# Mixture of experts: experts ranked by token count, the four smallest on 64 slots in plain float32, inputs fetched by indirect DMA

## The chip, the cores and the metric

One core of one Trainium2 chip runs the whole program. The metric is device time in microseconds for one execution, the median over several.

## The reference, cut to what matters

256 tokens of width 1024 go through two blocks of two layers each. All data is float32. What matters here is the second feed-forward part of the first block: a router picks 2 of 8 experts for each token, and each expert is a SwiGLU with 3584 hidden units.

```python
def moe_swiglu(h, router_w, router_b, w_gate, w_up, w_down):
    logits = h @ router_w + router_b
    top_vals, top_idx = lax.top_k(logits, 2)
    top_w = softmax(top_vals)
    combine = sum(one_hot(top_idx, 8) * top_w[..., None], axis=-2)
    y = 0
    for e in range(8):
        y = y + combine[..., e:e+1] * ((silu(h @ w_gate[e]) * (h @ w_up[e])) @ w_down[e])
    return y
```

The weights of one expert are 3 x 1024 x 3584 float32 numbers, 44.04 MB; those of all eight are 352 MB. The router's counts on the inputs that the reference draws (seed 0) are 66, 67, 71, 64, 49, 57, 54 and 84 tokens for experts 0 to 7, 512 in all.

The second block has a stream of its own over a context of 256 tokens. Its first layer does not depend on the first block, so it can be computed beside it.

## The kernel before, in words

The program is a set of generators ("tasks") that issue instructions; a scheduler then orders each engine's instructions by priority. The main stream has the key "lead", the context's first layer (task `B` in `plan`) the key "fill" with a far lower priority: what it issues fills the places where the lead is not ready. Each task takes its buffers from its own set of pools (`Res`). While `B` runs, the lead's experts use `RM`: four weight buffers w0, split buffers h0, h2 and w2, PSUM t0 and a0. `B` uses `RF`: w1, h1, PSUM a1 and t1. `plan` runs the expert generator until it yields "alone" and then gives it all weight buffers (`RN`); from there nothing fills. "alone" stands in the third expert (number 2), just before its last unit. So two and nine tenths experts run beside `B`, and five and one tenth after it.

The precise products are made of three passes. A weight tile arrives by one DMA of 512 KB (`wload`, L211, issued by the queue SP, 128 rows of 4 KB). `split` (L295) makes of it a rounded high part in float32r on ACT (L296) and the rest on DVE (L297). `mm3` (L228) then issues three float32r products: high x high (L234), high x low (L239), low x high (L240).

`moe` (L747) normalizes the tokens, computes the logits, picks the top two by vector operations, and ranks the tokens of each expert by products with a triangle of ones, which gives each token its slot (`pos`). If an expert has more than 128 tokens, the branch at L824 runs `overflow` for slots 128 and up. `experts` (L893) then takes the eight experts in their order. `gather(e)` makes one-hot matrices from the slots (L903), multiplies the normalized tokens by them (L909, plain float32, 16 products of 128 columns), applies scale and shift (L915, L917) and splits the result. `unit(u)` multiplies the 128 gathered slots (stationary) by 512 columns of gate and up weights over 8 blocks of k: 24 passes of 512 columns. 14 units make an expert; `down` adds 28 blocks of k times two column halves: 168 passes. With 14 x 24 that is 504 passes of 512 columns and 84 loads of 512 KB (56 for gate and up, 28 for down) for each expert. `scatter` (L882) adds the result to the tokens by a product with the one-hot rows.

Plain float32 is used elsewhere in the kernel: the modulation (L388, L410) and the convolution (L689) put four products of 32 output rows side by side on the column groups of TensorE. In the trace a plain float32 product has two records for each instruction of the program.

Of the kernel before, what the change touches and what calls it, by code (L numbers as in the profile page):

```python
# [9 lines left out]
F32 = mybir.dt.float32  # L10
F32R = mybir.dt.float32r
# [6 lines left out]
P = 128  # L18
D = 1024
T = 256  # L20
# [26 lines left out]
CC_SPEC = [("ident", 128), ("ones", 128), ("tri", 128), ("iota", 128), ("rev8", 8), ("psum", 32), ("pick1", 4), ("pick2", 8)]  # L47
# [15 lines left out]
class Res:  # L63
    """buffers of one stream: pools to take each kind of tile from (the listed ones in turn)"""
# [14 lines left out]
class Task:  # L79
    """a generator of instructions with its buffers and its place in the order of issue"""  # L80
# [15 lines left out]
class Builder:  # L96
    def __init__(self, tc, A, out, es, taps=None):
# [23 lines left out]
        self.RF = Res(w[1:2], h[1:2], a1, a1, a1, a1, t1, s1, s1, s1, s1, k[1], g[1], m[1])  # L121
        self.RM = Res(w[:1], hm, t0, a0, a0, a0, t2, s3, s2, s2, s3, k[0], g[0], m[0])
# [94 lines left out]
    def wparts(self, dram):  # L217
        """loads dram [128, kt, n]; yields (first k, its k count, high part, low part), 4 KiB a part"""
# [28 lines left out]
    def half_rsqrt(self, h, w):  # L247
        """1 / sqrt(2 h): three Newton steps, each of which turns the sign, from a negative guess"""
# [36 lines left out]
    def rstd_rows(self, xs):  # L285
        """xs[t][n] [128,512] token-major; 1/rms per token, [128, 1] for each t"""
# [24 lines left out]
    def affine_f32(self, ps, kp, Aff, Bff, pool=None):  # L311
        """ps [128, 2, w] -> A*ps+B"""
# [21 lines left out]
    def scaled_t(self, xs, r):  # L334
        """channel-major xs * r, two blocks of channels at a time: products with diagonals of r"""
# [18 lines left out]
    def conds(self):  # L354
        """silu of the three conditions, [128, 8, 32]: second block's two, first block's, zeros"""
# [16 lines left out]
    def gemv_step(self, m, c, A, name, l, grow):  # L372
        """a twelfth of the 6144 columns, in four column groups of the tensor engine"""
# [6 lines left out]
    def shift_scale(self, m, b, q, w_dram):  # L380
        """128 columns of each half of shift and scale: a column group each, then to channels on partitions"""
# [45 lines left out]
    def affine(self, m, which, i, gname):  # L427
        """(A, B) of g * (1 + scale), shift; which 0: mixer, 1: ffn"""
# [13 lines left out]
    def proj_parts(self, H, w, n, evac, kind="a"):  # L442
        """token-major [2 x 128, n] = H^T-stationary product with w [128, 8, n], in parts"""
# [19 lines left out]
    def ffn(self, H, gu, dn, nu, part, size=2):  # L463
        """SwiGLU over 256 tokens; part(section, t, n, psum) gets the product of each section of the hidden units"""
# [5 lines left out]
        def unit(u):  # L470
            """hidden units on partitions: gate and up blocks of 128, two of each to a bank"""
# [72 lines left out]
    def mixer1(self, l, H, M):  # L544
# [10 lines left out]
        # convolution branch, channels on partitions  # L555
# [30 lines left out]
        # gating branch  # L586
# [26 lines left out]
        # gating products  # L613
# [25 lines left out]
        # convolution, layer norm over channels, swish  # L639
# [107 lines left out]
    def moe(self, xs, m):  # L747
        nc, A = self.nc, self.A
        Aff, Bff = self.affine(m, 1, 0, "gf1")
        V, S, ones = nc.vector, nc.scalar, self.cc("ones")  # L750
# [7 lines left out]
        for t in range(2):  # L758
# [3 lines left out]
            V.tensor_add(lg[:, t], ps, rb)  # L762

# [39 lines left out]
        tri = self.cc("tri")  # L803
        for t in range(2):
# [6 lines left out]
        ps = self.ms(8)  # L811
        for t in range(2):
            nc.tensor.matmul(ps, ones, sel[:, t], start=t == 0, stop=t == 1)
        mx = self.m1(1)
        V.tensor_reduce(mx, ps, AX.X, ALU.max)
        cnt = cp.tile([P, 1], I32, name="cnt")
        V.tensor_copy(cnt, mx)
        self.tap("cw", cw)
        self.tap("pos", pos)
        G = [self.gate_bc(m, 5, 0, n) for n in range(2)]  # L820
        pos2 = cp.tile([P, 2, 8], F32, name="pos2")
        V.tensor_scalar(pos2, pos, 128.0, None, op0=ALU.subtract)
        nmax = nc.values_load(cnt[0:1, 0:1], min_val=0, max_val=256)
        with self.tc.If(nmax > 128):  # L824
            r, self.R = self.R, self.R0
            self.overflow(xn, Aff, Bff, pos2, cw, G, xs)
            self.R = r
        yield
        yield from self.experts(xn, Aff, Bff, pos, cw, G, xs)

    def overflow(self, xn, Aff, Bff, pos, cw, G, xs):
        """slots 128..255 of each expert, in the buffers of the weights alone"""
        nc, A = self.nc, self.A
        V, S, idn, iota = nc.vector, nc.scalar, self.cc("ident"), self.cc("iota")
        for e in range(8):
            mt = self.shaped(self.htile(), (8, 128))
            Dt, DT, act = mt[:, 0:2], mt[:, 2:4], mt[:, 4:8]
            Df = Dt.bitcast(F32)
            for t in range(2):
                V.tensor_scalar(Dt[:, t], iota, pos[:, t, e:e + 1], None, op0=ALU.is_equal)  # L840
            Xh, Xl = (self.shaped(self.tile(self.R.turn("w"), 1024, F32R), (8, 128)) for _ in range(2))
            for k in range(8):
                ps = self.tp(128)
                for t in range(2):
                    nc.tensor.matmul(ps, xn[t][k // 4][:, (k % 4) * 128:(k % 4 + 1) * 128], Df[:, t],
                                     start=t == 0, stop=t == 1)
                hf = self.g1(128)
                V.tensor_scalar(hf, ps, Aff[:, k:k + 1], Bff[:, k:k + 1], op0=ALU.mult, op1=ALU.add)
                self.split(Xh[:, k], Xl[:, k], hf)
            pd = self.tp(2, 128)  # L850
# [1027 lines left out]
```

## Time and profile before

| | us |
|---|---|
| median of three runs | 2912.77 (2910.46, 2912.77, 2920.75) |
| profiled execution: span | 2917.1 |
| PE busy | 2771.0 (95%) |
| DVE busy | 2025.3 (69%) |
| ACT busy | 1700.4 (58%) |
| DMA | 711.71 MB, mean 244 GB/s |

The page gives the span of the profiled execution, from its first to its last instruction, and no separate time for it; the span is 4.3 us over the median of the runs. PE is the matrix engine and PEld its weight loads, DVE the vector engine, ACT the scalar engine, POOL the general engine, SP the queue that issues loads. Records of products are about 0.17 us longer than the place they take on PE, since a product drains while the next one streams; the pace is read from their starts.

### The profile page before, as it was taken

The page shows a single profiled execution, that of the slowest core. Times are in us where ns is not written, and L with a number is a line of the kernel's source. Part 1 is how long each engine was busy: PE and PEld are TensorE (multiplying, and loading weights), DVE is VectorE, ACT ScalarE, POOL GpSimd, SP SyncE. Part 2 cuts the span into 40 slices and gives each one's busy share as a digit, 9 for nine tenths or more (in the row PEclk, how much of TensorE's full clock was granted, in tenths as well). Part 3 has the DMA queues.
Part 4 walks back from the last instruction along what each step waited for, and adds up shares of the span by engine and source line. Part 5 has one row for each costly group of instructions (what it writes and reads, how often), then busy time and mean ns, then how long its engine had stood idle before and what let it go on. Part 6 is the DMA issues. An engine that isn't in the chain of part 4 may idle for free.

```text
span 2917.1 us, 46050 instructions
## 1 busy us (share of the span) xinstructions
PE 2771.0 (95%) x17334; PEld 2295.3 (79%) x17334; DVE 2025.3 (69%) x3099; ACT 1700.4 (58%) x2353; POOL 77.8 (3%) x144
## 2 busy tenths in 40 slices
PE   6999999998899999999999999998999999799898
PEld 5767788776788888887878888876667989677897
DVE  3535555656777878789899998985566555666555
ACT  3435445545566666666777777775445554654543
POOL 0110000010000000000000000000000000000000
PEclk8999999999999999999999999999989999899999
DMA  9987766642688888888999999996563556324463
GB/s 358 338 298 234 250 198 225 222 127 84 224 307 296 295 282 299 298 290 313 350 354 339 350 347 360 355 361 210 167 211 110 182 171 189 118 66 132 152 185 112
DMA packets 202954, 711.71 MB, mean 244 GB/s; under 512 B 24506, under 2 KB 28730, under 8 KB 202720
## 3 DMA queue, kind: packets, MB, share of 16 engines
q1 hardware_dynamic: 196112, 692.82, 69.6%
q0 software_dynamic: 6320, 15.30, 1.8%
q8 instruction: 138, 2.26, 0.3%
q14 instruction: 96, 0.79, 0.1%
q10 hardware_dynamic: 288, 0.55, 0.1%
HBM read 704.49 MB, written 4.08 MB: 243 GB/s over the span
## 4 chain that ended last, share of the span: by engine, by line
PE 65%; DVE 3%; ACT 2%; DMA 2%; issue 1%; DVEq 0%; SPq 0%; ACTq 0%; POOLq 0%
PE a0t L234 8%; PE a0t L239 8%; PE a0t L240 8%; PE a1t L239 6%; PE a1t L240 6%; PE a1t L234 6%; PE t0t L239 5%; PE t0t L240 5%; PE t0t L234 5%; PE a1t L1512 1%; PE t0t L1535 1%; ACT h0t L296 1%; DVE h0t L297 1%; PE t0t L344 1%; PE t2t L909 1%
## 5 line engine op out<-in xcount | busy, mean ns | idle before, releaser
L296 ACT CAST h0t<-w0t 128x1024 fp32r<-128x1024 f32 (+1 forms) x505 | 525.4, 1043 | 386.1 <-PE a0t L239 243.8
L297 DVE TENSOR_TENSOR h0t<-w0t,h0t 128x1024 fp32r<-128x1024 f32 (+1 forms) x302 | 364.9, 1209 | 264.7 <-ACT h0t L296 247.5
L234 PE MATMUL a0t<-s0t,h0t 128*128 128x256 f32 x800 | 225.9, 287 | 4.4 <-ACT h0t L296 2.1
L239 PE MATMUL a0t<-s0t,h0t 128*128 128x256 f32 x800 | 224.2, 284 | 0.0
L240 PE MATMUL a0t<-s0t,h0t 128*128 128x256 f32 x800 | 220.1, 286 | 0.5 <-DVE h0t L297 0.5
L296 ACT CAST h1t<-w1t 128x1024 fp32r<-128x1024 f32 x155 | 162.9, 1051 | 96.1 <-PE a1t L239 44.6
L239 PE MATMUL a0t<-h0t,s2t 128*128 128x512 f32 x492 | 193.8, 396 | 0.0
L240 PE MATMUL a0t<-h0t,s2t 128*128 128x512 f32 x466 | 181.0, 394 | 0.0
L297 DVE TENSOR_TENSOR h2t<-w0t,h0t 128x1024 fp32r<-128x1024 f32 x122 | 149.1, 1222 | 29.9 <-ACT h0t L296 22.3
L234 PE MATMUL a0t<-h0t,s2t 128*128 128x512 f32 x466 | 167.4, 399 | 1.0 <-DVE s0t L1176 0.5
L234 PEld LDWEIGHTS a0t<-s0t,h0t 128*128 128x128 f32 x800 | 153.0, 192 | 13.1 <-issue 4.5
L296 ACT CAST h0t<-w1t 128x1024 fp32r<-128x1024 f32 x120 | 126.2, 1052 | 49.4 <-PE a1t L240 17.4
L239 PEld LDWEIGHTS a0t<-s0t,h0t 128*128 128x128 f32 x800 | 153.6, 192 | 1.6 <-issue 0.8
L240 PEld LDWEIGHTS a0t<-s0t,h0t 128*128 128x128 f32 x800 | 150.0, 192 | 4.2 <-DVE h0t L297 1.9
L234 PE MATMUL t0t<-h0t,s0t 128*128 128x512 f32 x374 | 147.1, 393 | 1.9 <-ACT h0t L296 1.9
L239 PE MATMUL t0t<-h0t,s0t 128*128 128x512 f32 x372 | 147.7, 397 | 1.3 <-DVE h0t L297 1.3
L240 PE MATMUL t0t<-h0t,s0t 128*128 128x512 f32 x374 | 147.5, 394 | 0.0
L297 DVE TENSOR_TENSOR h1t<-w0t,h0t 128x1024 fp32r<-128x1024 f32 x81 | 98.9, 1221 | 25.1 <-ACT k0t L483 6.6
L297 DVE TENSOR_TENSOR h1t<-w1t,h1t 128x1024 fp32r<-128x1024 f32 x80 | 97.7, 1222 | 23.9 <-ACT h1t L296 21.8
L239 PE MATMUL a1t<-s1t,h1t 128*128 128x256 f32 x408 | 113.7, 283 | 0.0
L234 PE MATMUL a1t<-s1t,h1t 128*128 128x256 f32 x408 | 113.4, 283 | 0.0
L297 DVE TENSOR_TENSOR h0t<-w0t,h1t 128x1024 fp32r<-128x1024 f32 x80 | 97.7, 1221 | 20.0 <-ACT k0t L483 5.0
(740 smaller groups left out, 7453.2 us busy)
## 6 DMA issues: line engine op xcount, KB each, us to landing
w0t<-in_mgu_dram SPq DMA_DIRECT2D x306, 512.0 KB, 5.5
w0t<-in_mdn_dram SPq DMA_DIRECT2D x152, 512.0 KB, 5.2
w1t<-in_mgu_dram SPq DMA_DIRECT2D x107, 512.0 KB, 5.7
w0t<-in_f2gu_dram SPq DMA_DIRECT2D x66, 512.0 KB, 3.9
w1t<-in_f2gu_dram SPq DMA_DIRECT2D x61, 512.0 KB, 4.8
w1t<-in_win_dram SPq DMA_DIRECT2D x54, 512.0 KB, 4.9
w1t<-in_mdn_dram SPq DMA_DIRECT2D x54, 512.0 KB, 5.4
w1t<-in_mod_s_dram SPq DMA_DIRECT2D x48, 512.0 KB, 6.2
```

Of the source, the lines that this page charges most:

```text
L234: i = mm(ps, lh, rh, start=start if skip else first, stop=False, skip_group_check=skip)
L239: mm(ps, lh, rl, start=False, stop=False, skip_group_check=skip)
L240: mm(ps, ll, rh, start=False, stop=last, skip_group_check=skip)
L296: self.nc.scalar.copy(out_h, src)
L297: self.nc.vector.tensor_sub(out_l, src, out_h)
L344: self.nc.tensor.matmul(ps[:, q, t * 128:(t + 1) * 128], xs[t][k // 4][:, (k % 4) * 128:(k % 4 + 1) * 128], dg[:, t], start=True, stop=True)
L909: nc.tensor.matmul(ps[:, q], xn[t][k0 // 4][:, q * 128:q * 128 + 128], Dt[:, t], start=t == 0, stop=t == 1)
L1512: nc.tensor.matmul(pe[:, h].rearrange("p a b -> p (a b)"), x[:, (h0 + h) * 128:(h0 + h + 1) * 128], rhs, start=i == 0, stop=i == 1)
L1535: nc.tensor.matmul(ps[:, h], L[:, h], R[:, h], start=True, stop=True)
```

## The change

The count of each expert is computed first, and the experts are put in order of their counts (a rank by comparing 8 x 8 numbers; the expert's own number breaks ties). Slots and weights are permuted into that order. The eight expert numbers go to eight registers of SP, and every expert load takes its address from such a register. Whatever has more tokens than its place allows (64 for the first four, 128 for the others) goes to the overflow branch.

The inputs are no longer gathered by one-hot products. The affine result of all tokens (`keep`) is transposed back to rows, stored to DRAM, and each expert fetches its rows by an indirect DMA on POOL, with the token numbers as indices. `G2` is the output gate in two halves of 64 partitions.

The four smallest experts (`expert64`) use plain float32 products with no split. Their 64 slots are the stationary operand; two blocks of 512 columns go at the same time to output partitions 0 to 63 and 64 to 127. Their loads go in turn to w0 and h0, four buffers each (`RS`). "alone" now stands before the fifth expert. The other four (`expert128`) are `unit` and `down` as before, with register addresses.

```diff
+        self.RS = Res([w[0], h[0]], h[:1], t0, a0, a0, a0, t2 + a0, s3, s2, s2, s3, k[0], g[0], m[0])
...
     def moe(self, xs, m):
-        r = self.rstd_rows(xs)
-        keep = [self.affine_f32(ps, kp, Aff, Bff, self.xpools[0]) for kp, ps in enumerate(self.scaled_t(xs, r))]
-        xn = self.xnorm(xs, r, self.xpools[0])
+        keep = [self.affine_f32(ps, kp, Aff, Bff, self.xpools[0])
+                for kp, ps in enumerate(self.scaled_t(xs, self.rstd_rows(xs)))]
...
+        self.hrow = [self.dram(T) for _ in range(2)]
+        for t in range(2):
+            for n in range(2):
+                ps = self.tp(4, 128)
+                for q in range(4):
+                    k = 4 * n + q
+                    nc.tensor.transpose(ps[:, q], keep[k // 2][:, k % 2, t * 128:t * 128 + 128], idn)
+                y = self.s2(4, 128, pool=self.xpools[0])
+                if n:
+                    S.copy(y, ps)
+                else:
+                    V.tensor_copy(y, ps)
+                nc.gpsimd.dma_start(self.hrow[n][t * 128:t * 128 + 128], y.rearrange("p a b -> p (a b)"))
...
+        V.scalar_tensor_tensor(n8, pc, 8.0, self.cc("rev8"), op0=ALU.mult, op1=ALU.subtract)
+        V.tensor_tensor(less, n8[:, None, :].to_broadcast(b8), n8[:, :, None].to_broadcast(b8), op=ALU.is_lt)
+        V.tensor_reduce(rank, less, AX.X, ALU.add)
+        V.tensor_tensor(perm, rank[:, None, :].to_broadcast(b8), i8[:, :, None].to_broadcast(b8), op=ALU.is_equal)
+        def ranked(out, v):
+            V.tensor_tensor(j, perm, v[:, None, :].to_broadcast(b8), op=ALU.mult)
+            V.tensor_reduce(out, j, AX.X, ALU.add)
+        ranked(f8, i8)
+        V.tensor_copy(eid, f8)
+        ranked(c8, cnt8)
+        V.tensor_sub(c8, c8, caps)
...
+            ranked(pos_r[:, t], pos[:, t])
+            ranked(cwt[:, t, :, 0], cw[:, t])
...
+        _, eids = nc.values_load_multi_w_load_instructions(eid[0:1, 0:8], engines=(mybir.EngineType.SP,), min_val=0, max_val=7)
+        nmax = nc.values_load(cnt[0:1, 0:1], min_val=0, max_val=512)
         with self.tc.If(nmax > 128):
+            self.overflow(eids, pos2, cwt, G, xs)
...
+    def slots(self, pos, cwt, r, width, Dt=None):
+        for t in range(2):
+            V.tensor_scalar(o, i0, pos[:, t, r:r + 1], None, op0=ALU.is_equal)
+        for t in range(2):
+            nc.tensor.matmul(pw, Dt[:, t].bitcast(F32), cwt[:, t, r], start=t == 0, stop=t == 1)
...
+    def fetch(self, out, n, idx):
+        self.nc.gpsimd.indirect_dma_start(out=out, out_offset=None, in_=self.hrow[n][:, :],
+            in_offset=bass.IndirectOffsetOnAxis(ap=idx[:out.shape[0]], axis=0))
...
+    def inputs64(self, idx):
+        for n in range(2):
+            g = self.s2(512)[:64]
+            self.fetch(g, n, idx)
+            for q in range(4):
+                self.nc.tensor.transpose(ps[:, 4 * n + q], g[:, q * 128:q * 128 + 128], self.cc("ident")[:64, :64])
+        self.nc.scalar.copy(X, ps)
...
+    def expert64(self, reg, X):
+        gu, dn = self.expert("mgu", reg), self.expert("mdn", reg)
+        def units(p):
+            ps = self.acc(512)
+            for k0 in range(0, 8, 2):
+                w = [self.wload(gu(2 * p + g, slice(None), slice(k0, k0 + 2))) for g in range(2)]
+                for j in range(2):
+                    for g in range(2):
+                        nc.tensor.matmul(ps[64 * g:64 * g + 64], X[:, k0 + j], w[g][:, j],
+                                         start=k0 + j == 0, stop=k0 + j == 7)
+            a = self.glu_evac(ps)
+...
+        def down(p):
+            for i in range(4):
+                w = self.wload(dn(slice(None), slice(k, k + 1)))
+                for n in range(2):
+                    nc.tensor.matmul(pn[0][64 * n:64 * n + 64], act[p][:, q, 64 * g:64 * g + 64],
+                                     w[:, 0, n * 512:n * 512 + 512], start=k == 0, stop=k == 27)
+        for p in range(7):
+            units(p)
+            if p: down(p - 1)
+            if p == 3: yield "next"
+        down(6)
...
-        moe = task(self.moe(xs, m[1]), RM)
+        moe = task(self.moe(xs, m[1]), self.RS)
```

In `experts`, `if r == 4: yield "alone"` stands where the test for expert 2 stood. `ranked(c8, cnt8)` gives the counts in the new order. `slots` makes the one-hot rows of a rank and from them the weight and the token number of each slot. The label "next" is where the next expert's slots and inputs are issued. The scatter of a small expert is one weighted copy of 512 columns and four plain float32 products on 64 rows.

## Rows read from the trace of the kernel before

**Rows 1.** Windows: us, then busy us (records) by engine, granted clock, DMA share, GB/s.
```profile
757.00:1303.00 546.00, 542.15 (x2978) 468.95 (x2979) 435.62 (x494) 365.87 (x452) 0.00 (x0) 0.99 0.87 293
1303.00:1330.00 27.00, 23.20 (x97) 18.71 (x96) 22.00 (x29) 16.16 (x24) 1.07 (x2) 0.94 0.84 280
1330.00:1951.00 621.00, 615.42 (x2821) 502.06 (x2820) 571.17 (x647) 475.38 (x590) 0.00 (x0) 1.00 0.96 350
```

**Rows 2.** DMA issues from 757 to 1303: count, KB each, us to landing.
```profile
w0t<-in_mgu_dram SPq DMA_DIRECT2D x164, 512.0 KB, 5.4
w0t<-in_mdn_dram SPq DMA_DIRECT2D x79, 512.0 KB, 4.9
w1t<-in_f2gu_dram SPq DMA_DIRECT2D x40, 512.0 KB, 5.5
w1t<-in_f2dn_dram SPq DMA_DIRECT2D x22, 512.0 KB, 5.0
```

**Rows 3.** Groups by form, 757 to 1303: the context stream's passes, one of three lines each.
```profile
L239 PE MATMUL a1t<-s1t,h1t 128*128 128x256 f32 x352 | 97.8, 283 | 0.0
L239 PE MATMUL a1t<-h1t,s1t 128*128 128x512 f32 x76 | 29.8, 392 | 0.7 <-DVE h1t L297 0.7
```

**Rows 4.** Timeline of PE: start, us, instruction; split passes at 320 and at 1500.
```profile
319.82 0.28 PE L239 MATMUL a0t<-s0t,h0t 128*128 128x256 f32 x1
319.94 0.28 PE L240 MATMUL a0t<-s0t,h0t 128*128 128x256 f32 x1
...
1499.84 0.39 PE L239 MATMUL a1t<-h2t,s0t 128*128 128x512 f32 x1
1500.07 0.39 PE L240 MATMUL a1t<-h0t,s0t 128*128 128x512 f32 x1
```

**Rows 5.** Timeline of PE from 2194: plain float32 over the whole width.
```profile
2194.37 1.98 PE L1625 MATMUL t0t<-k0t,s1t 128*128 128x512 f32 x4
2196.19 0.38 PE L1575 MATMUL t1t<-s1t,s0t 128*128 128x128 f32 x2
```

**Rows 6.** Windows, records of L689 alone: four column groups in plain float32.
```profile
640.00:650.00 10.00, 9.99 (x150) 5.70 (x138) 1.00 0.63 194
```

**Rows 7.** Timeline of PE from 2043: column groups between whole-width passes.
```profile
2043.86 0.39 PE L240 MATMUL a0t<-h0t,s1t 128*128 128x512 f32 x1
2044.09 0.61 PE L234 MATMUL a0t<-h0t,s1t 128*128 128x512 f32 x2
2044.63 0.64 PE L410 MATMUL a1t<-w1t,conds 128*32 128x256 f32 x8
2045.20 0.50 PE L239 MATMUL a0t<-h1t,s1t 128*128 128x512 f32 x1
2045.54 0.39 PE L240 MATMUL a0t<-h0t,s1t 128*128 128x512 f32 x1
2045.77 0.39 PE L234 MATMUL a0t<-h0t,s1t 128*128 128x512 f32 x1
```

**Rows 8.** Windows, 20 to 40 us.
```profile
20.00:40.00 20.00, 15.65 (x181) 10.40 (x184) 5.11 (x29) 3.06 (x9) 0.00 (x0) 0.51 1.03 408
```

**Rows 9.** Waits of the queue SP, 757 to 1303: total us, times, longest.
```profile
SPq L211 <- DVE h0t L297: 170.2, 118, 4.0
SPq L211 <- DVE h2t L297: 107.8, 76, 3.5
```

**Rows 10.** Lines L211 and L823 on SP: duration ns min/median/max.
```profile
L211 SPq DMA_DIRECT2D w0t<-in_mgu_dram x164: 327/328/949, 757.0 to 1292.9; - x164
L823 SPq TENSOR_LOAD <-cnt x1: 464/464/464, 749.8 to 749.8; - x1
L823 SPq FUSED_REGOPS  x1: 186/186/186, 750.3 to 750.3; - x1
```

**Rows 11.** Timeline of DVE at 741: two operations of the router.
```profile
741.49 0.17 DVE L799 TENSOR_TENSOR m0t<-m0t,m0t 128x16 f32<-128x16 f32 x1
741.82 0.18 DVE L801 TENSOR_TENSOR cw<-cw,m0t 128x16 f32<-128x16 f32 x1
```

**Rows 12.** DMA issues of the whole span on POOL's queue.
```profile
s0t<-dt POOLq DMA_DIRECT2D x10, 256.0 KB, 4.0
dt<-s3t POOLq DMA_DIRECT2D x4, 256.0 KB, 5.0
```

**Rows 13.** Chain of waits, 757 to 1303: start, us, half of one gather.
```profile
866.19 1.78 PE t2t L909 x16
```

More of the change, by code (lines that the diff above doesn't have):

```diff
@@ L824, in moe @@
+        _, eids = nc.values_load_multi_w_load_instructions(
+            eid[0:1, 0:8], engines=(mybir.EngineType.SP,), min_val=0, max_val=7,
+            skip_runtime_bounds_check_because="the experts' numbers in another order")
+        nmax = nc.values_load(cnt[0:1, 0:1], min_val=0, max_val=512)
         with self.tc.If(nmax > 128):
             r, self.R = self.R, self.R0
-            self.overflow(xn, Aff, Bff, pos2, cw, G, xs)
+            self.overflow(eids, pos2, cwt, G, xs)
             self.R = r
@@ L828, in moe, with expert @@
         yield
[L829 to L835, printed above, removed]
+        yield from self.experts(eids, pos_r, cwt, G, G2, xs)
+    def expert(self, name, reg):
+        w = self.A[name]
+        return lambda *i: w[(bass.ds(reg, 1), *i)].rearrange("o p k n -> (o p) k n")
+    def slots(self, pos, cwt, r, width, Dt=None):
+        nc, V = self.nc, self.nc.vector
+        Dt = self.s2(2, 128) if Dt is None else Dt
+        i0 = self.cc("iota")[:, 0:width]
+        for t in range(2):
+            o = Dt[:, t]
+            if width == 64:
+                o = o.rearrange("p (a b) -> p a b", a=2)
+                i0 = self.cc("iota")[:, None, 0:64].to_broadcast([P, 2, 64])
+            V.tensor_scalar(o, i0, pos[:, t, r:r + 1], None, op0=ALU.is_equal)
+        pw = self.tp(2)
+        for t in range(2):
+            nc.tensor.matmul(pw, Dt[:, t].bitcast(F32), cwt[:, t, r], start=t == 0, stop=t == 1)
+        w = self.m1(3)
+        V.tensor_copy(w[:, 0:1], pw[:, 0:1])
+        V.tensor_scalar(w[:, 1:2], pw[:, 1:2], 1.0, None, op0=ALU.subtract)
+        V.tensor_scalar(w[:, 2:3], pw[:, 1:2], 129.0, None, op0=ALU.subtract)
+        idx = self.m1(1, I32)
+        V.tensor_scalar(idx, pw[:, 1:2], 1.0, 0.0, op0=ALU.subtract, op1=ALU.max)
+        return w, idx
@@ new lines, in rows_at, with overflow @@
+    def rows_at(self, DT, w):
+        for t in range(2):
+            self.nc.vector.tensor_scalar(DT[:, t], self.cc("iota"), w[:, 1 + t:2 + t], None, op0=ALU.is_equal)
+    def fetch(self, out, n, idx):
+        self.nc.gpsimd.indirect_dma_start(
+            out=out, out_offset=None, in_=self.hrow[n][:, :],
+            in_offset=bass.IndirectOffsetOnAxis(ap=idx[:out.shape[0]], axis=0))
+    def overflow(self, eids, pos, cwt, G, xs):
+        nc = self.nc
+        V, S, idn = nc.vector, nc.scalar, self.cc("ident")
+        for r in range(8):
+            gu, dn = self.expert("mgu", eids[r]), self.expert("mdn", eids[r])
@@ L836, in overflow @@
             mt = self.shaped(self.htile(), (8, 128))
[L837 to L840, printed above, removed]
+            DT, act = mt[:, 2:4], mt[:, 4:8]
+            w, idx = self.slots(pos, cwt, r, 128, mt[:, 0:2])
+            self.rows_at(DT, w)
+            Xg = self.wtile()
             Xh, Xl = (self.shaped(self.tile(self.R.turn("w"), 1024, F32R), (8, 128)) for _ in range(2))
[L842 to L849, printed above, removed]
@@ new lines, in experts, with ready @@
+    def experts(self, eids, pos, cwt, G, G2, xs):
+        def ready(r):
+            small = r < 4
+            w, idx = self.slots(pos, cwt, r, 64 if small else 128)
+            DT = self.s2(2, 128, dt=F32 if small else F32R)
+            self.rows_at(DT, w)
+            return (self.inputs64 if small else self.inputs128)(idx), DT, w[:, 0:1]
+        nxt = ready(0)
+        for r in range(8):
+            if r == 4:
+                yield "alone"
+            X, DT, ws = nxt
+            steps = self.expert64(eids[r], X) if r < 4 else self.expert128(eids[r], X)
+            for at in steps:
+                if at == "next":
+                    if r < 7:
+                        nxt = ready(r + 1)
+                elif at is None:
+                    yield
+                else:
+                    pn = at
+            if r < 4:
+                y = self.s2(512)
+                self.nc.vector.scalar_tensor_tensor(y, pn, ws, G2, op0=ALU.mult, op1=ALU.mult)
+                for t in range(2):
+                    for n in range(2):
+                        ps, sl = self.ms(512), slice(64 * n, 64 * n + 64)
+                        self.nc.tensor.matmul(ps, DT[sl, t], y[sl], start=True, stop=True)
+                        self.nc.vector.tensor_add(xs[t][n], ps, xs[t][n])
+            else:
+                for n in range(2):
+                    yh, yl = self.st(512, dt=F32R), self.st(512, dt=F32R)
+                    self.scatter(pn[n], ws, G[n], self.s2(512), yh, yl, DT, xs, n)
+            yield
@@ L978, in experts @@
             yield
+            if p == 3:
+                yield "next"
+        down(6)
+        yield pn
     def setup(self):
```

205 lines of the change are left out of this document (107 added, 98 removed).

## The prediction

> **What bounds the kernel now.** I read the windows first, since the change touches one stretch only. From 757 us, where the first expert load is issued, to 1303, where the second mode with all buffers begins, PE is busy for 542 of 546 us, DMA 0.87 of its time and DVE 436 us [rows 1]. So the stretch in which the context stream fills the gaps of the experts is bound by PE. From 1330 to 1951 PE is busy for 615 of 621 us, DMA 0.96 and DVE 571: PE first, with DMA and DVE close behind [rows 1]. The DMA issues say what each stretch carries: 243 expert loads (164 and 79) and 62 of the context up to 1303 [rows 2]. Of the 672 loads of eight experts (84 each) 429 are left for the 648 us from 1303 to 1951: 1.51 us a load, 127 us an expert. The waits of SP show the loads waiting mostly for the DVE half of a split, which frees the weight buffer [rows 9]: the loads follow the products, not the other way round. Everything outside 757 to 1951 stays as it is.
>
> I go through three stretches: the router, stage 1 (experts beside the context stream) and stage 2 (experts alone). The sum is made against the profiled execution's 2917.1 us. That is 4.3 us, or 0.15%, over the median of 2912.8, and I take the difference over to the median. About 0.5%, 15 us, is what a measurement of this kernel can tell from no change.
>
> **Router.** Before SP can load an expert number, the change adds a chain of about 8 small DVE operations (comparison, two reductions, permutation, copies) at 0.18 us with their gaps 0.2 each [rows 11]: 1.6 us. The check of the counts, slots and weights in the new order add some 16, 3.2 us, on the same in-order engine. Eight register loads on SP at 0.46 [rows 10] would be 3.7 us. Sixteen transposes at 0.11 (16 records in 1.78 us [rows 13]) are 1.8 us of PE, and four copies lie beside them on DVE and ACT. The four scalings of the normalized tokens go. The ends are 2 us, if the chain lies beside the transposes, and 15, if all is in series; I take 7: loads begin at 764. The first inputs need a row store (5.0 us) and then a fetch (the direct read of a row in DRAM takes 4.0 us [rows 12]). An indirect one is not in the trace; between 4 and 10 us. During it up to eight weight buffers fill, 4 MB or some 11 us of DMA, so it costs nothing while the loads stay the bound; without that cover at most 10 us, once. Later fetches are issued half an expert ahead. POOL is idle throughout both stages but for two issues [rows 1].
>
> **Stage 1, DMA.** It now carries four experts and the same context work: 336 + 62 = 398 loads, 208.7 MB. The loads of a small expert have eight buffers, and these are freed by products instead of splits. At the 350 GB/s of the stretch from 1330, divided by its share 0.96 [rows 1], DMA gives 365 GB/s: 572 us. The ends are 596 us at 350 itself, and 527 us at 396 (408 GB/s at a share of 1.03 from 20 to 40 us [rows 8], where many loads stand ready). I take 572: the same weights in the same 4 KB rows.
>
> **Stage 1, PE.** A split product of 512 columns is paced at 0.227 us a pass, one of 256 at 0.12 [rows 4]. The context has 3 x 352 of 256 and 3 x 76 of 512 [rows 3]: 127 + 52 = 179 us. A big expert would need 504 x 0.227 = 114 us. A small one has 112 + 56 = 168 plain float32 products. The trace shows these at full width: four records, two products, from 2194.37 to 2196.19 [rows 5], 0.91 us each. One alone would make 168 x 0.91 = 153 us, more than the split expert. All hangs on whether the two column halves run at once. No row has halves of 64, but the convolution has quarters of 32: 150 records of 256 columns in 10 us, 67 ns each [rows 6], against 228 if one came after another (half of 455 [rows 5]). So 3.4 of 4 run at once. The bounds for an expert are then 76 us (two at once) and 153 (one after another); I take 80, near the row with the quarters. Four make 320 us. Transposes and scatter add about 26 products' records at 0.11 and four at 0.91, 6.5 us an expert, 26 in all. PE: 320 + 179 + 26 = 525 us, under the 572 of DMA.
>
> One rule speaks against the change. Where a batch of eight column records stands between whole-width passes, the stretch from 2044.63 to 2045.54 holds 0.46 us of column work (two rounds of 0.228) and one pass of 0.227 [rows 7]: 0.22 us are left over. The Trainium skill, "TensorEngine Tiling (Array Packing)", section "Key Properties", says that a change of the tiling mode, not only of the tile, drains TensorE; the row agrees. A small expert comes in 28 groups for gate and up and 28 for down, so at most 56 such excursions, 12 us an expert and 49 in all. By the row PE then needs 525 to 574 us.
>
> ACT and DVE lose 84 splits an expert at about 1.05 and 1.22 us, and neither was first here; the release of their time counts for nothing beyond the loads that no longer wait for it. What is late next is DMA, with PE right behind. Two engines within 10% of their bound don't cover each other wholly: I take 590 us for stage 1, 18 above the DMA term.
>
> **Stage 2.** Four big experts at 127 us are 508. Each loses its gather of 32 records at 0.11 (3.6 us) for eight transposes (0.9): 2.7 us of a PE that is 99% busy, 11 in all; nothing if DMA takes over, which at 365 GB/s needs 121 us an expert. I take 497. The loads' register addresses cost SP perhaps three register operations of 0.19 beside the issue of 0.33 [rows 10], about 1.0 us with a wait, below 1.48 (590 / 398) and 1.5 us: hidden.
>
> **Sum.** Last expert load at 764 + 590 + 497 = 1851 instead of 1951: 100 us less. Forecast 2817 for the profiled execution, 2813 for the median.
>
> **Rivals.** First, the fill bunches up. The order on PE's queue is written ahead, and lead products go first. If the schedule takes the small experts for busier on PE than they are, the context's work is put late, and from the fifth expert on the lead needs w1, h1 and a1, which the context holds until its end. The lead's own 176 MB take 483 us; with all 179 us of the context behind them stage 1 is 662, with half of it (527 us of loads, then 90) 617. Time 2840 to 2885; 2865 as one number. For it: two streams with a fixed order; against it: before, the context's passes run through the whole of stage 1 with PE 99% busy [rows 1]. Second, stage 1 goes better: loads at the 396 GB/s [rows 8] and few excursions, 540 us, 2763. For it: eight buffers and no split in the way; against it: PE needs 525 without any switch.
>
> Third, the other side: the halves run one after another, as [rows 5]. Then PE needs 4 x 153 + 179 + 26 = 817 us in stage 1, the end is 127 us later, 3040. It decides above 0.72 us a product (1951 - 764 - 497 = 690; less 205, over 672 products), between the 0.48 taken and 0.91. For it: no row has halves; against it: [rows 6]. Fourth, SP: at 2 us a load instead of 1.0, 398 and 336 loads need 796 and 672 us, about 3190; against it [rows 10]. Fifth, the change doesn't keep to its places: the reference's four smallest counts are 49, 54, 57 and 64, so the fourth is full. One token more by another rounding, and the branch runs all experts again: 8 x 127 = 1016 us more, over 3800.
>
> **How the numbers follow.** Forecast 0.57 (its own range 2785 to 2840), bunched fill 0.20, better 0.10, halves in series 0.07, SP 0.02, overflow 0.02, and 0.02 for no change by pieces of these. Faster by over 0.5%: 0.87; within: 0.02; slower: 0.11. The range for 8 in 10 leaves out the slower cases: 2765 to 2885.
>
> **What will show it.** Right: pairs of 64-column records that start within some ns of each other, and a pace near 0.46 us for a pair of passes; DMA share in stage 1 at 0.95 or more at 350 to 380 GB/s, SP waiting for PE instead of DVE; the first load of the fifth expert near 1355; the context's passes spread up to that point; stage 2 at 124 us an expert. Wrong: column records in series; a stretch before the fifth expert in which only the context's passes run while DMA idles; SP issuing back to back with no waits; expert loads after the eighth expert.

## The result, and the profile after

| | us |
|---|---|
| before, median of 4 runs beside the changed kernel | 2911.61 (2909.69 to 2920.75) |
| after, median of 4 runs | 2845.28 (2842.21 to 2845.92) |
| ratio | 0.9762, 95% interval 0.9747 to 0.9778 |
| forecast | 2813 (2765 to 2885) |
| span of the profiled execution after | 2844.0 |

The change saves 66 us where 100 were forecast, and the time is 32 us above the forecast of 2813. It lies 5 us above the forecast's own range (2785 to 2840) and inside the interval of the first rival (2840 to 2885). To find the 32 us, look first at when each expert's first load is issued, since the loads follow the products. These times are the starts of the load instructions in the trace:

| first load of expert, us | 1 | 2 | 3 | 4 | 5 | 6 | 7 | 8 | last load |
|---|---|---|---|---|---|---|---|---|---|
| before | 757 | 935 | 1129 | 1322 | 1452 | 1578 | 1704 | 1831 | 1951 |
| after | 757 | 932 | 1128 | 1278 | 1387 | 1512 | 1637 | 1761 | 1882 |

Stage 1 (from 757 to the first load of the fifth expert) took 630 us, 40 more than forecast. Stage 2 took 495 (forecast 497), and the loads began at 757, not 764. So the whole miss lies in stage 1: 2813 + 40 - 2 - 7 = 2844.

The windows of the changed kernel answer to [rows 1]. The columns are the same: us, busy us (records) of PE, PEld, DVE, ACT and POOL, granted clock, DMA share, GB/s.

```profile
757.00:1215.00 458.00, 451.34 (x2215) 243.46 (x2217) 127.86 (x186) 103.21 (x143) 7.96 (x8) 0.99 0.89 309
1215.00:1388.00 173.00, 161.78 (x598) 48.97 (x596) 24.03 (x57) 14.28 (x35) 3.12 (x4) 1.00 1.01 393
1388.00:1882.00 494.00, 486.80 (x2166) 386.04 (x2165) 444.61 (x497) 366.32 (x451) 12.45 (x6) 1.00 0.98 362
```

Stage 1 has two parts with different bounds. Up to 1215 the context runs beside the small experts, PE is busy for 451 of 458 us and DMA has room (0.89). The context's last product comes at 1227; from there the small experts are by themselves, and DMA is full (1.01). DMA was forecast to bound the whole of stage 1. It bounds only the end of it; PE bounds the rest, as before the change (the run e1_pair below shows it).

What PE does in that time is read from the timeline (start us, duration, engine, line, instruction). L1052 is the gate and up product of a small expert; `w0t` and `h0t` hold the weights of its two column halves. L236, L241 and L242 are the three passes of a split product (the lines 234, 239 and 240 of before). The first line is the indirect fetch on POOL (L923).

```profile
759.74 1.01 POOL L923 DMA_INDIRECT s3t<-dt,m0t  x1 [10.04 <-DVE m1t L278]
...
773.18 0.64 PE L1052 MATMUL t0t<-w0t,s0t 128*64 128x512 f32 x1 [0.24 <-ACT s0t L1024]
773.18 0.64 PE L1052 MATMUL t0t<-h0t,s0t 128*64 128x512 f32 x1
773.66 0.59 PE L1052 MATMUL t0t<-w0t,s0t 128*64 128x512 f32 x1
773.66 0.59 PE L1052 MATMUL t0t<-h0t,s0t 128*64 128x512 f32 x1
774.09 0.59 PE L1052 MATMUL t0t<-w0t,s0t 128*64 128x512 f32 x1
774.09 0.59 PE L1052 MATMUL t0t<-h0t,s0t 128*64 128x512 f32 x1
...
1002.80 0.59 PE L1052 MATMUL t0t<-h0t,s0t 128*64 128x512 f32 x1
1002.81 0.59 PE L1052 MATMUL t0t<-w0t,s0t 128*64 128x512 f32 x1
1003.23 1.02 PE L1052 MATMUL t0t<-h0t,s0t 128*64 128x512 f32 x2
1004.18 0.39 PE L241 MATMUL a1t<-s1t,h1t 128*128 128x256 f32 x1
1004.40 0.28 PE L242 MATMUL a1t<-s1t,h1t 128*128 128x256 f32 x1
1004.61 0.64 PE L1052 MATMUL t0t<-w0t,s0t 128*64 128x512 f32 x1
1004.62 0.64 PE L1052 MATMUL t0t<-h0t,s0t 128*64 128x512 f32 x1
```

At 773.18 the reader sees what the forecast hoped for: the two halves start at the same time, within some ns, the next pair 0.48 us later and the one behind it 0.43. I call one such pair of records a round. At 1003.23 there is what it did not foresee: two records of `h0t` run with no partner, for two rounds' time (1003.23 to 1004.18, 0.43 each and the change of tiles at the end), and then two passes of the context follow. A half alone takes as long as both together. I count two records as one round when they start within 0.1 us of each other. Stage 1 then has 798 rounds, of which 252 hold one half; if all 1344 records ran in pairs there would be 672.

The lone halves have two sources. Of the 252, 140 lie before 1215. The order of PE's instructions is written ahead, and in it a context product stands between a half and its partner: after 130 of these 140 the next other work on PE is a pass of the context. The other 112 come later, when the loads bound and PE waits for the load of one half (waits of PE, 1215 to 1388: total us, times, longest):

```profile
PE t0t L1052 <- DMA h0t<-in_mgu_dram: 6.3, 26, 0.7
```

As forecast, the loads now wait mostly for products and hardly for the split on DVE. These waits of the queue SP from 757 to 1215 answer to [rows 9] (total us, times, longest):

```profile
SPq L213 <- PE t0t L1052: 202.3, 100, 11.5
SPq L213 <- PE a0t L1069: 65.6, 51, 3.2
SPq L213 <- DVE h1t L299: 16.9, 11, 3.5
```

An expert's load with its address in a register costs SP little. The instructions at L213, 757 to 1388 (count, ns min/median/max), answer to [rows 10]:

```profile
L213 SPq FUSED_REGOPS  x338: 43/46/51, 757.3 to 1387.9; - x169
L213 SPq DMA_DIRECT2D w0t<-in_mgu_dram x113: 332/333/453, 756.8 to 1386.9; - x113
L213 SPq MOVE w0t<-in_mgu_dram x113: 29/29/37, 758.9 to 1388.0; - x113
```

That is 333 + 46 + 29 = 408 ns, where a load before took 328 [rows 10].

The indirect fetch, which had no row before, is among the DMA issues (KB not shown; us to landing):

```profile
s3t<-dt,m0t POOLq DMA_INDIRECT x16, 7.5
```

### The profile page after: what moved, and what is told of

Its sections match the earlier page's. It is cut to its first block, busy times and chain, and to the rows that moved or that the text cites. A ratio compares the mean times of both kernels' runs of the same rounds, so it can differ in the third digit from the quotient of the medians.

```text
span 2844.0 us, 44057 instructions
## 1 busy us (share of the span) xinstructions
PE 2684.3 (94%) x16414; PEld 1980.1 (70%) x16414; DVE 1594.7 (56%) x2691; ACT 1322.7 (47%) x1909; POOL 103.5 (4%) x166
## 4 chain that ended last, share of the span: by engine, by line
PE 49%; DMA 5%; DVE 3%; ACT 3%; issue 1%; SPq 0%; DVEq 0%; ACTq 0%; POOL 0%; POOLq 0%
PE a0t L236 7%; PE a0t L241 6%; PE a0t L242 6%; PE a1t L241 4%; PE a1t L242 4%; PE a1t L236 4%; DMA h0t<-in_mgu_dram 3%; PE t0t L1052 3%; PE t0t L241 2%; PE t0t L236 2%; PE t0t L242 2%; PE a0t L1069 1%; PE a1t L1660 1%; DVE h0t L299 1%; PE t0t L1683 1%
## 5 line engine op out<-in xcount | busy, mean ns | idle before, releaser
L298 ACT CAST h0t<-w0t 128x1024 fp32r<-128x1024 f32 (+1 forms) x316 | 327.7, 1038 | 307.0 <-PE a0t L241 220.0
L299 DVE TENSOR_TENSOR h0t<-w0t,h0t 128x1024 fp32r<-128x1024 f32 (+1 forms) x214 | 257.1, 1203 | 230.9 <-ACT h0t L298 214.1
L236 PE MATMUL a0t<-s0t,h0t 128*128 128x256 f32 x800 | 225.9, 287 | 4.7 <-ACT h0t L298 2.4
L1052 PE MATMUL t0t<-w0t,s0t 128*64 128x512 f32 x448 | 227.6, 610 | 2.2 <-DMA w0t<-in_mgu_dram 2.0
L241 PE MATMUL a0t<-s0t,h0t 128*128 128x256 f32 x800 | 224.3, 284 | 0.0
L1052 PE MATMUL t0t<-h0t,s0t 128*64 128x512 f32 x448 | 214.2, 604 | 6.7 <-DMA h0t<-in_mgu_dram 6.3
L242 PE MATMUL a0t<-s0t,h0t 128*128 128x256 f32 x800 | 220.1, 286 | 0.4 <-DVE h0t L299 0.4
L236 PEld LDWEIGHTS a0t<-s0t,h0t 128*128 128x128 f32 x800 | 153.0, 192 | 13.3 <-issue 4.5
L241 PEld LDWEIGHTS a0t<-s0t,h0t 128*128 128x128 f32 x800 | 153.5, 192 | 1.6 <-issue 0.8
L242 PEld LDWEIGHTS a0t<-s0t,h0t 128*128 128x128 f32 x800 | 149.9, 192 | 4.2 <-DVE h0t L299 1.9
L241 PE MATMUL a0t<-h0t,s2t 128*128 128x512 f32 x352 | 139.8, 398 | 0.0
L298 ACT CAST h0t<-w1t 128x1024 fp32r<-128x1024 f32 x101 | 106.0, 1050 | 40.2 <-PE a1t L242 17.0
L242 PE MATMUL a0t<-h0t,s2t 128*128 128x512 f32 x308 | 120.0, 391 | 0.0
L236 PE MATMUL a1t<-s1t,h1t 128*128 128x256 f32 x408 | 118.9, 296 | 0.0
L1052 PEld LDWEIGHTS t0t<-h0t,s0t 128*64 128x64 f32 x448 | 52.9, 136 | 94.0 <-issue 54.2
L241 PE MATMUL a1t<-s1t,h1t 128*128 128x256 f32 x408 | 114.6, 285 | 0.0
L236 PE MATMUL a0t<-h0t,s2t 128*128 128x512 f32 x308 | 112.5, 401 | 1.1 <-DVE s0t L542 0.3
L242 PE MATMUL a1t<-s1t,h1t 128*128 128x256 f32 x396 | 109.5, 294 | 0.3 <-DVE h1t L299 0.3
L462 DVE TENSOR_TENSOR g0t<-t0t,g0t 128x256 f32<-128x256 f32 x56 | 23.5, 420 | 147.2 <-ACT g0t L460 146.2
L460 ACT ACTIVATE g0t<-t0t 128x256 f32<-128x256 f32 x56 | 21.5, 384 | 180.9 <-PE t0t L1052 171.4
```

What stands on the lines that cost most here:

```text
L236: i = mm(ps, lh, rh, start=start if skip else first, stop=False, skip_group_check=skip)
L241: mm(ps, lh, rl, start=False, stop=False, skip_group_check=skip)
L242: mm(ps, ll, rh, start=False, stop=last, skip_group_check=skip)
L298: self.nc.scalar.copy(out_h, src)
L299: self.nc.vector.tensor_sub(out_l, src, out_h)
L460: self.nc.scalar.activation(sg, ps[:, :256], AF.Silu)
```

## The experiments

Theory A: stage 1 lost its 40 us because PE bounds it while the context runs, and PE lost time to halves without a partner and to changes between 64-column and whole-width tiles. Theory B: the loads bound stage 1, whatever PE does. The letters in the texts quoted below are each run's own. In each run the earlier kernel was timed beside it on the same chip; the ratio is to that.

**Both halves together (e1_pair).** The first product of each group of four is made to wait for the second of the two loads, so that the scheduler cannot issue one half before the other is ready:

```diff
-        self.nc.sync.dma_start(v, dram)
+        self.dma = self.nc.sync.dma_start(v, dram)
...
-                        nc.tensor.matmul(ps[64 * g:64 * g + 64], X[:, k0 + j], w[g][:, j],
-                                         start=k0 + j == 0, stop=k0 + j == 7)
+                        i = nc.tensor.matmul(ps[64 * g:64 * g + 64], X[:, k0 + j], w[g][:, j],
+                                             start=k0 + j == 0, stop=k0 + j == 7)
+                        if j + g == 0:
+                            self.tc.add_manual_dep(i.ins, self.dma.ins.name, LATE, reason="both halves together")
...
```

> The changed kernel, but the first product of each group of four waits for both loads, so that the two column halves stand together in PE's order. Theory A (PE bounds the small experts while the context runs; 140 rounds there hold one half alone, 0.43 us each, two of them where one would do): rounds with one half fall below 20 up to the context's end, that part gets 25 to 30 us shorter, the part after it stays bound by DMA at about 405 GB/s; 2815 to 2822 us. Rival B (the loads bound this part, a lone half only fills a wait for its partner's load): no change, 2841 to 2849.

Measured: 2802.68 us, ratio 0.9606 (0.9585 to 0.9628), beyond what A gave. The trace has 676 rounds, 8 of them with one half. Its windows:

```profile
757.00:1177.00 420.00, 414.47 (x2217) 235.91 (x2218) 125.72 (x183) 102.02 (x142) 7.94 (x8) 0.99 0.94 340
1177.00:1345.00 168.00, 139.84 (x590) 44.65 (x589) 24.97 (x58) 14.15 (x34) 3.13 (x4) 0.99 1.01 395
1345.00:1840.00 495.00, 488.78 (x2177) 387.47 (x2173) 445.44 (x498) 368.15 (x454) 9.93 (x6) 1.00 0.98 363
```

Stage 1 is 589 us (first load of the fifth expert at 1345), 41 less; stage 2 is unchanged. PE's busy time in stage 1 falls from 451 + 162 = 613 to 414 + 140 = 554, 59 us; 122 rounds fewer at 0.429 us are 52. Not all 59 us come out at the end, since the last 168 us are bound by the loads.

The two parts tell which of it counted. While the context runs, PE's busy time falls by 37 us (451 to 414) and the time by 38 (458 to 420). There the lone halves fall from 140 to 8; two of them make one full round, so that is 66 rounds or 28 us. The changes between 64-column and whole-width tiles fall from 141 to 115 as well, which is 9 us at the price worked out below. In the last part PE's busy time falls by 22 us (162 to 140), and the time by only 5 (173 to 168). So the halves that the context parts from their partners, with the changes of tiles that come with them, are shown to be the miss; A fell short because it counted the halves alone.

The same trace prices a change of tiles:

```profile
1003.16 0.28 PE L241 MATMUL a1t<-s1t,h1t 128*128 128x256 f32 x1
1003.28 0.28 PE L242 MATMUL a1t<-s1t,h1t 128*128 128x256 f32 x1
1003.49 0.64 PE L1052 MATMUL t0t<-w0t,s0t 128*64 128x512 f32 x1
...
1003.97 0.59 PE L1052 MATMUL t0t<-w0t,s0t 128*64 128x512 f32 x1
...
1004.40 0.59 PE L1052 MATMUL t0t<-w0t,s0t 128*64 128x512 f32 x1
...
1004.83 0.59 PE L1052 MATMUL t0t<-w0t,s0t 128*64 128x512 f32 x1
...
1005.36 0.73 PE L236 MATMUL a1t<-h1t,s1t 128*128 128x512 f32 x2
1005.93 0.41 PE L241 MATMUL a1t<-h1t,s1t 128*128 128x512 f32 x1
```

I call a stay in the 64-column tiles, from going in to going out, an excursion. Going in, the step of 0.12 us becomes 0.21 (1003.28 to 1003.49) and the first round takes 0.48 instead of 0.43; going out, the last round takes 0.53 (1004.83 to 1005.36) and the next two passes 0.57 instead of 2 x 0.227 [rows 4]. Together 0.09 + 0.05 + 0.10 + 0.12 = 0.36 us for one excursion. The medians over this run's excursions between context passes are the same four: 0.21, 0.48, 0.53 and 0.57 us. Stage 1 of the changed kernel has 162 excursions, this run 136.

**One half after the other (e2_serial).** For gate and up the loop over the halves is put outside, so they mostly run alone:

```diff
-            for k0 in range(0, 8, 2):
-                w = [self.wload(gu(2 * p + g, slice(None), slice(k0, k0 + 2))) for g in range(2)]
-                for j in range(2):
-                    for g in range(2):
+            for g in range(2):
+                for k0 in range(0, 8, 2):
+                    w = self.wload(gu(2 * p + g, slice(None), slice(k0, k0 + 2)))
+                    for j in range(2):
...
```

> The changed kernel with the loop over the two halves put outside, so that of gate and up the eight products of one half stand before the eight of the other; down is left as it is. Theory A (two halves at once are what pays): 448 products at 0.86 us instead of 0.43 each, so PE needs 384 + 96 + 185 for the context + 65 for switches and the rest = 730 us in stage 1 instead of 594; stage 1 735 to 765, in all 2950 to 2980, slower than before the change. Rival B (the loads bound it): below 2880.

Measured: 2952.17, ratio 1.0107 (1.0083 to 1.0131), as A has it. There are 1056 rounds, 768 with one half, and PE is the bound for longer:

```profile
760.00:1372.00 612.00, 606.00 (x2440) 294.01 (x2441) 135.07 (x195) 108.39 (x154) 8.44 (x10) 0.99 0.82 273
1372.00:1496.00 124.00, 117.47 (x370) 38.62 (x370) 17.22 (x47) 8.59 (x23) 1.98 (x2) 1.00 0.96 352
```

With the changed kernel and the run before, stage 1 rises with the rounds: 676, 798 and 1056 of them give 589, 630 and 736 us, 0.34 us for each round more and then 0.41. The second slope is nearly a round's own time (0.429), for here DMA has room (0.82). This is also rival 3 made in earnest for the gate and up products: without pairs the change would have cost time.

**No small experts (e4_all128).** All eight experts run as `expert128`, 128 slots and split products, in the new order with registers and fetch; "alone" stands where it stood before:

```diff
-        V.memset(caps[:, 0:4], 64.0)
-        V.memset(caps[:, 4:8], 128.0)
+        V.memset(caps, 128.0)
...
-            small = r < 4
+            small = False
...
-        moe = task(self.moe(xs, m[1]), self.RS)
+        moe = task(self.moe(xs, m[1]), self.RM)
```

> Ranking, registers and the fetch by indirect DMA as in the changed kernel, but all eight experts on 128 slots with split weights, in the buffers and with the place of the second mode of the kernel before. Theory A (the gain is the small experts' products): 8 gathers less at 2.7 us, some lost at the start since the first inputs come later; 2890 to 2905. Rival C (the gather's removal and the ranking are what pays): 2845 to 2870. Rival D (register addresses or the fetch cost something that the small experts hide): above 2915.

Measured: 2919.4 against 2915.0, ratio 1.0011 (0.9999 to 1.0023): no change; A had 2890 to 2905, and only D's bound (above 2915) is met. The windows are cut at the first load of the fifth expert:

```profile
757.00:1460.00 703.00, 679.48 (x3508) 571.79 (x3508) 563.73 (x649) 466.02 (x566) 14.21 (x12) 0.99 0.87 301
1460.00:1955.00 495.00, 490.02 (x2190) 394.48 (x2191) 455.13 (x510) 373.57 (x461) 13.89 (x6) 1.00 0.97 359
```

The second part is 5 us shorter than before (495 against 1951.5 - 1451.8 = 500), the first 8 us longer (1460 against 1452). One wait of POOL's fetch for the slots is 11.5 us long at the start of it; which part of the 8 us is due to it was not taken apart. So order, registers and fetch are worth nothing together, and the 66 us come from the small experts.

**The context spread out (e5_spread).** As e1_pair, and the context's steps are spread over the small experts: the first load of each is tied to a small product further on.

```diff
-        B.run()
         moe.run("alone")
+        n = 0
+        while B.at != "end":
+            k = int((n - 2) * 1.12)
+            if 0 <= k < len(self.marks):
+                self.hold = self.marks[k]
+            B.step()
+            self.hold = None
+            n += 1
...
```

> e1_pair, and in addition the first load of each part of the context is held back until a given product of the small experts has begun, so that the context's work lasts until late in the fourth expert. Theory A (context and small experts together leave DMA at 0.89 of its time for 458 us, and then DMA alone bounds 173 us in which PE has nothing to fill with): with both spread evenly stage 1 is PE's 541 us plus 15 to 35; 2770 to 2795. Rival E (the place of the context's work doesn't matter, only its sum): as e1_pair, within 8 us.

Measured: 2796.09, ratio 0.9579 (0.9558 to 0.9600); by the expectations' own bounds this is the rival's result (within 8 us of e1_pair). The context now ends at 1263, and stage 1 is 582 us instead of 589:

```profile
758.00:1263.00 505.00, 488.11 (x2545) 264.58 (x2546) 140.61 (x206) 110.81 (x161) 8.44 (x10) 0.98 0.95 352
1263.00:1340.00 77.00, 61.66 (x266) 18.79 (x265) 11.52 (x37) 5.93 (x15) 1.98 (x2) 1.00 1.03 409
```

The time bound by loads alone shrinks from 168 to 77 us, but the longer first part has PE at 97%: there was little idle time to win.

**Bursts (e3_burst and e6_burst_spread).** To have fewer changes of tiles, four loads are gathered before eight rounds, on e1_pair and on e5_spread:

```diff
-            for k0 in range(0, 8, 2):
-                w = [self.wload(gu(2 * p + g, slice(None), slice(k0, k0 + 2))) for g in range(2)]
-                for j in range(2):
+            for k0 in range(0, 8, 4):
+                w = [self.wload(gu(2 * p + g, slice(None), slice(k0 + k1, k0 + k1 + 2))) for k1 in (0, 2) for g in range(2)]
+                for j in range(4):
...
```

> As the run with the two halves together (2802.7 us), but with four loads of one small expert gathered before eight rounds of products, so that TensorE goes over to 64-column tiles less often: about 109 excursions in the written order where that run had 137. A (the change of tiles costs TensorE about 0.3 us each time, and TensorE is the bound while the context's feed-forward runs beside): 28 excursions x 0.3 = 8 us less, 2793 to 2797 us; first stage of the loads 580 instead of 589. B (the loads are the bound on the whole of the stage by now): no difference, 2800 to 2806. C (a burst waits for the last of four loads and gives back four of the buffers at once, so the queue of loads stands while TensorE works through it): 2808 to 2830, with waits of the load queue for TensorE of more than 20 us in sum beyond those of that run.

> The same bursts of four loads on the run in which the context's feed-forward was spread over the small experts (2796.1 us). A (excursions cost TensorE 0.3 us each and TensorE bounds): 2785 to 2792 us, first stage 573 to 578 instead of 582. B (what is left of the first stage is the loads: 398 loads x 0.524 MB = 208.7 MB at the 405 GB/s of the lead alone is 515 us, at the 350 GB/s that were had beside the context 596 us): no difference, 2793 to 2799. C (bursts stop the queue of loads): 2803 to 2830.

Measured: 2820.43 (ratio 0.9668, 0.9654 to 0.9682) and 2826.52 (0.9680, 0.9666 to 0.9695): the times of C in both. There are indeed 109 excursions and no lone half, but stage 1 is 610 and 609 us. Windows of e3_burst, cut where its context ends:

```profile
758.00:1279.00 521.00, 486.60 (x2537) 265.77 (x2537) 137.97 (x204) 111.12 (x160) 9.35 (x10) 0.99 0.95 341
1279.00:1368.00 89.00, 66.83 (x273) 22.81 (x271) 12.92 (x39) 6.25 (x16) 1.98 (x2) 0.92 0.96 356
```

Neither engine is full any more: PE is at 93%, then at 75%, and even alone the small experts get 356 GB/s instead of 395 (e1_pair) or 409 (e5_spread). A burst holds four of the eight buffers until it begins. Between bursts PE goes through the context faster than its weights are split (waits of PE, 780 to 1279):

```profile
PE a1t L236 <- ACT h1t L298: 26.6, 28, 1.0
```

and the queue of loads then stands for the context's buffers too. These are its waits in e3_burst up to its context's end (758 to 1279):

```profile
SPq L213 <- DVE h1t L299: 139.9, 37, 5.5
SPq L213 <- PE t0t L1052: 102.6, 80, 11.7
```

and in e1_pair (757 to 1177):

```profile
SPq L213 <- PE t0t L1052: 170.7, 63, 12.6
SPq L213 <- DVE h1t L299: 14.6, 8, 5.1
```

So the sign that C named, over 20 us more of waits for TensorE, did not come: those waits fell, and the waits for the split on DVE rose by 125 us. The time of C was met with another wait than the one it named.

What an excursion costs is therefore not shown by a run of its own. PE's busy time over stage 1 is 553.4 us here against 554.3, for 27 excursions fewer, but the gaps at a change of tiles are not counted as busy, and the waits moved.

**No context (e8_noctx).** `B.run()` is left out of e1_pair: the rest of the context's feed-forward is not computed, so the small experts have the loads to themselves.

> The run with the two halves together (2802.7 us, first stage of the loads 589 us), with the rest of the context's feed-forward left out (so the context's part of the result is not the reference's, and the later layers get a context stream without it): the small experts have the loads to themselves. A (beside the context TensorE was the bound, and the loads alone bound the small experts): 336 loads x 0.524 MB = 176.2 MB at the 405 to 409 GB/s that the small experts had once the context was done is 431 to 435 us; first stage 430 to 445, total 2640 to 2660. B (the small experts' own products bound at about the pace of the loads: 672 rounds x 0.4285 = 288 us and their change-overs, well below): would show as TensorE over 95% busy in the stage and more than 450 us. C (the loads, not TensorE, bounded the stage with the context too): 398 loads against 336 at one rate, 589 x 336 / 398 = 497 us, total 2705 to 2715.

Measured: 2661.19 (two runs, 2653.90 and 2668.48), stage 1 445 us: at the upper end of A (430 to 445; the time 1 us above its 2660), and far from C's 497.

```profile
756.00:1201.00 445.00, 348.32 (x1456) 103.09 (x1456) 29.78 (x85) 25.47 (x62) 9.41 (x10) 0.97 1.01 397
```

Now DMA is full from end to end at 397 GB/s, and PE is busy for 78%. At that rate the 208.7 MB of stage 1 would be 526 us: DMA alone does not account for the 589 of e1_pair, where PE's 554 do nearly. Whether the loads could reach 397 GB/s with the context beside them is not shown: the most that any run has there is 352 (e5_spread, share 0.95).

**Plain rows for the first expert (e9_first_rows).** In e1_pair, the first expert takes the first 64 tokens by plain transfers issued ahead of the branch, so its result is not the reference's.

```diff
+        self.X0 = self.inputs64(None)
         with self.tc.If(nmax > 128):
...
+            if idx is not None:
                 self.fetch(g, n, idx)
+            else:
+                self.nc.gpsimd.dma_start(g, self.hrow[n][0:64, :])
...
```

> The run with the two halves together (2802.7 us), but the first small expert takes the first 64 tokens, fetched by two plain transfers ahead of the branch, instead of its own tokens by their numbers (so that expert's result is not the reference's): its inputs are ready when its loads land. A (the inputs that come late, 10 us of TensorE at the stage's start, are lost for good, because TensorE is the bound while the context runs): first product near 762 to 765 instead of 772, first stage 578 to 582 instead of 589, total 2792 to 2796. B (the loads run ahead meanwhile and TensorE catches up, as it has slack at the end of the stage, where the loads alone bound): 2799 to 2806.

Measured: 2801.43, ratio 0.9613 (0.9600 to 0.9627), the same as e1_pair: B by the time. The first product comes at 768 instead of 772, and the first load of the fifth expert at 1346 instead of 1345. The test is weaker than meant, since the loads themselves began at 761 instead of 756 here; with the loads that far behind, the product waited for them (3.6 us) and not for its inputs.

Of the two versions that beat both kernels, e5_spread has the lower median (2796.09) and e1_pair the simpler edit (2802.68); their intervals overlap.

## Why the prediction was right in direction and 32 us short

**Router.** Forecast 7 us, measured none: loads began at 757 in both kernels. The first inputs came late, as the prediction allowed: the fetch waited 10.04 us for the slots, and the first product came at 773, where before one came at 762. The condition under which this was to cost nothing (the loads being the bound) did not hold, but PE had context passes to run: of the first 18 us (757 to 775) it idled 6.

**Stage 1, PE: the step that failed.** "Two at once" was right. The 0.72 us a product as the point that decides was too high: e2_serial has 1056 x 0.429 / 672 = 0.67 us a product and is already slower than the kernel before. The sum took for granted that all products pair. Its terms, with what they measured over stage 1:

| term | forecast us | measured us | from |
|---|---|---|---|
| 672 rounds | 320 | 288 | 0.429 a round instead of 0.476 |
| halves without a partner | not seen | 54 | 798 - 672 = 126 rounds more; 70 of them (30 us) before 1215 |
| changes of tiles | 0 to 49 | 58 | 162 x 0.36 instead of up to 224 x 0.22 |
| context | 179 | 187 | 1056 x 0.12 + 264 x 0.227; the window of [rows 3] ends before the last 36 of the 264 |
| transposes, scatter | 26 | (26) | taken over, not measured apart |
| sum | 525 to 574 | 613 | busy 613 |

The term that is missing is the one that makes the difference: without it, the same sum gives 559, and e1_pair, which takes it away, has PE at 554 busy and stage 1 at 589, where the forecast had 590. The price of an excursion was mis-sized too, 0.36 us against 0.22. The 18 us that the forecast added, because two engines near their bounds don't cover each other wholly, had no row behind it; measured, stage 1 is 17 us longer than PE is busy in it (630 and 613). The row with four quarters [rows 6] showed that parts can run at once; it stood in a stretch where nothing else was ready to come between them. Here another stream was, and the order in which PE gets the instructions decides.

The rule of the Trainium skill that the prediction weighed ("TensorEngine Tiling (Array Packing)", section "Key Properties": a change of tiling mode drains TensorE) agrees with the trace, at 0.36 us for going in and out rather than the 0.22 of [rows 7].

**Stage 1, DMA: mis-sized, and not the bound.** 365 GB/s was taken; the small experts alone get 393 to 409, near the upper of the two ends [rows 8]. At the 397 of e8_noctx the term would be 526 us and not 572; beside the context no run shows that rate. That error hid the first: had DMA been priced so and PE as above, PE would have stood out as the bound. The forecast's 590 is met by e1_pair with other parts, 420 us bound by PE and 168 by loads; that is luck in the number and not the mechanism that was forecast. The Trainium skill, "Perfetto Trace Analysis", section "Roofline", puts a single core's ceiling at about 435 GB/s, by its 16 DMA engines, rather than at its share of 358; the 409 GB/s at a share of 1.03 agree with the first of these.

**Stage 2 and SP.** Right: 495 for 497, and the four big experts at 124.7 us each (1387 to 1761 for three). SP's price was lower than taken, 0.41 us a load instead of 1.0.

**The rivals.** The first (context bunched late) has the measured time in its interval, but its mechanism went the other way: the context ran early, ended at 1227, and PE was short of time before it and not after it. What it names as its ground, an order written ahead for two streams, did cost the time, by parting the halves. The third fell with the pairs at 773.18 and stands measured in e2_serial. The fourth falls with 0.41 us a load, the fifth with 672 expert loads, the last at 1882. The second did not come about; e5_spread is the nearest, with 582 us of stage 1 against its 540.

## What to carry to other kernels

Where two column halves are to run at once, price them by the order in which TensorE gets them: here a half that was issued without its partner cost as much as both (0.429 us), and the order worked out ahead parted them where another stream had work ready. Tie the pair to the later of its two loads, and count rounds in the trace by their starts. Price each stretch with each engine's best measured rate; an average taken from a stretch bound by another engine can hide which one is next, as 365 GB/s did here.

## What was not expected of the hardware

- The indirect fetch of 64 or 128 rows takes 7.5 us from issue to landing while weights are loaded, a plain transfer on the same queue 4.0 [rows 12].
- A plain float32 product of 512 columns on 64 output columns leaves nearly as long a mark as on all 128: 0.429 us a record here, 0.455 at full width [rows 5].
- Gathering loads in larger groups, with the buffers as many as before, cost 18 us (e3_burst against e1_pair) and 30 (e6_burst_spread against e5_spread), though it left no half without its partner.
